# A mixer, cross-attention and expert layer on one core: nine gathered rows in flight where four were, and a pace of 0.7 beside the projections

## The chip, the cores and the metric

The kernel runs on one core of a Trainium2 chip. The metric is the device time of one launch in microseconds (us). Where a text below speaks of "no change", it means a difference of under 0.3%, about 13 us, which is what repeated measurements of this kernel can tell apart.

## The reference

One encoder layer is applied to two groups of tokens, 256 and 1024 of them, with a model width of 1024, all in float32:

```
x = x + W_out [ BiRetention(xn) ; MLA(xn) ]        # xn = RMSNorm(x), one input projection
x = x + MemCrossAttn(RMSNorm(x), RMSNorm(mem))     # 4 heads over 256 memory tokens
x = x + PEER(RMSNorm(x));  y = RMSNorm(x)

def blk(xt):                                        # PEER, for 128 tokens
    q = (xt @ wq).reshape(128, 8, 256)              # 8 heads
    s1, s2 = scores of the two halves of q against 128 sub-keys each
    ...                                             # top 16 of each, top 16 of their sums
    ids, g = the 8 * 16 chosen experts of each token, their softmax
    a = einsum('td,ted->te', xt, U[ids])            # 16384 experts: one row of U, one of V
    return einsum('te,ted->td', g * gelu(a), V[ids])
```

Each token has 128 chosen experts, and each expert is one row of 1024 numbers in U (`peer_u`) and one in V (`peer_v`).

## The kernel before

The 1280 tokens are ten tiles of 128. The stages follow one another: `phase_a` (input projection and retention of all tiles), `phase_b` for the first token block (tiles 0 and 1), with `phase_m` (latent attention) in it, `phase_m` for the second group, `phase_b` for the second and third token block (four tiles each: output projection, cross-attention, expert queries and scores), `gates`, `dense`.

The expert layer is computed in two ways. For six tiles (`DENSE`), `dense` runs over all 16384 experts in 128 blocks of 128 experts. For each block `a_stage` loads the block's rows of U (tiles `ur`, two loads of 256 KB) and V (`vr`, two loads), splits each into a high and a low part (`uh` and `vh` on ScalarE, `ul` and `vl` on GpSimd, four GpSimd instructions a block), multiplies U with the tokens into the PSUM tile `pa` (48 matmuls), applies Gelu (`wr`) and a table of gates (`gt`, 768 KB for two blocks) and splits the result (`wh`, `wl`); every three blocks (`NG`) `v_stage` multiplies it with V into `pv` (36 matmuls a block) and VectorE adds `pv` to `dacc`. The loads `ur` and `vr` share four buffers and are issued by the SP queue.

For the other four tiles (`GATHER`: 0, 1, 8, 9) the generator `gather` fetches just the chosen rows. One step is one indirect DMA issued by GpSimd, which brings one row of U for each of the 128 tokens into a tile `grow` of 128 x 1024 numbers (512 KB), and one VectorE instruction: for U a multiplication with the tokens (`gx`) whose row sum goes to `ga`, for V a multiplication by `ga` and addition to an accumulator. A tile has 128 steps on U and 128 on V, so there are 1024 steps in all. `grow` has four buffers: the fifth row can only be fetched when the first has been used. Once `dense` runs (`self.gps` is set), `banks` copies the tokens and the accumulator to PSUM (tile `gps`); before that they lie in SBUF (`gx`, `gacc`).

What sets the order: `routing` (top 16 lists, VectorE) and `gathering` are queues of generators. `tick(us)` is called behind each group of matmuls with its length and takes steps of them at a share `RHO`: the first number of a pair while there is routing left, the second for gathering. The three pairs belong to the projections (from `phase_m` of the second group on), to `gates` and to `dense`. What is left after `dense` is emitted behind it and depends only on the beginning of `dense`; the scheduler, which runs when the program is built, then sorts instructions of each engine into one fixed order by its own estimate of when each is ready and fits. So the number of buffers of `grow` enters the order of every engine. On the chip each engine follows its order strictly: an instruction that waits holds up all that stand behind it.

The pool `rp` holds the tiles of the routing, the pool `gp` those of the gathering.

Of the kernel before, what the change touches and what calls it, by code (L numbers as in the profile page):

```python
# [10 lines left out]
F32 = mybir.dt.float32  # L11
F32R = mybir.dt.float32r
BF = mybir.dt.bfloat16
# [8 lines left out]
P = 128  # L22
D = 1024
# [23 lines left out]
NG = 3  # L47
O1_BY = "va"

RHO = ((0.75, 0.42), (0.5, 0.0), (0.9, 0.0))  # L50
LATE = 2


SYNC = mybir.DependencyInfo(mybir.DependencyClass.Sync, mybir.DependencyReason.DATA)
# [7 lines left out]
class Lead:  # L62


    def __init__(self, k):
        self.k = k
# [39 lines left out]
class K:  # L106
    def __init__(self, nc, tc, I, O, dbg=None):
        self.nc, self.tc, self.I, self.O = nc, tc, I, O
        self.dbg = dbg or {}
        self.n = 0  # L110
        self.routing, self.gathering = [], []
        self.keeps = []
        self.spare = ()
        self.routed = set()
        self.owed, self.rho = 0.0, (0.0, 0.0)
        self.gps = None
        self.anchor = None
        self.v, self.vf = Lead(self), Fill(self)

    def tick(self, us):  # L120


        rho = self.rho[0 if self.routing else 1]
        if self.rho is RHO[1] and self.routed.issuperset(DENSE):
            rho = 0.0
# [7 lines left out]
    def step(self, q=None):  # L133
        q = q or self.routing or self.gathering
        try:
            return next(q[0])
        except StopIteration:
            q.pop(0)
            return 0.0

    def pace(self, r, ins=None):
# [156 lines left out]
    def phase_a(self, sd):  # L298
# [3 lines left out]
        with ExitStack() as es:  # L302
# [20 lines left out]
            with ExitStack() as e2:  # L323
# [16 lines left out]
                for p in range(RH // 2):  # L340
# [9 lines left out]
                    for t in tiles:  # L350
# [12 lines left out]
                        nc.gpsimd.tensor_tensor(gg[t], gg[t], gw, ALU.mult)  # L363
                        if p and t == LATE:
                            finish()
# [620 lines left out]
    def gather(self, gp, sd, t):  # L986

        nc, I = self.nc, self.I
        v = self.vf

        def row():
            return gp.tile([P, D], F32, tag="grow", name=self.nm("grow"), bufs=4)
        ids = gp.tile([P, P], I32, tag="gids", name=self.nm("gids"), bufs=2)
        nc.sync.dma_start(ids, sd["ids"][t])
        g = gp.tile([P, P], F32, tag="gg", name=self.nm("gg"), bufs=2)
        nc.sync.dma_start(g, sd["g"][t])
        x3 = gp.tile([P, D], F32, tag="gx", name=self.nm("gx"), bufs=1)
        nc.sync.dma_start(x3, sd["x3"][t])
        fw = row()
        nc.sync.dma_start(fw, I["norm_ffn_w"].partition_broadcast(P))  # L1000
        v.tensor_tensor(x3, x3, fw, ALU.mult)
        x3 = self.banks(x3)
        a = gp.tile([P, P], F32, tag="ga", name=self.nm("ga"), bufs=2)

        def rows(src, s):
            u = row()
            nc.gpsimd.indirect_dma_start(out=u, out_offset=None, in_=src,  # L1007
                                         in_offset=bass.IndirectOffsetOnAxis(ap=ids[:, s:s + 1], axis=0))
            return u
        for s in range(P):  # L1010
            u = rows(I["peer_u"], s)
            junk = gp.tile([P, D], BF, tag="gj", name=self.nm("gj"), bufs=1)
            v.scalar_tensor_tensor(junk, u, 1.0, x3, ALU.mult, ALU.mult, accum_out=a[:, s:s + 1])
            yield 1.2
        nc.scalar.activation(a, a, AF.Gelu)
        v.tensor_tensor(a, a, g, ALU.mult)
        acc = gp.tile([P, D], F32, tag="gacc", name=self.nm("gacc"), bufs=1)
        nc.sync.dma_start(acc, sd["x2"][t])
        out, acc = acc, self.banks(acc)
        for s in range(P):  # L1020
            u = rows(I["peer_v"], s)
            v.scalar_tensor_tensor(acc, u, a[:, s:s + 1], acc, ALU.mult, ALU.add)
            yield 1.2
        w = row()
        nc.sync.dma_start(w, I["final_norm_w"].partition_broadcast(P))
        self.finish(gp, t, acc, w, gp.tile([P, D], BF, tag="gj", name=self.nm("gj"), bufs=1), out)

    def banks(self, x):

# [184 lines left out]
    def run(self):  # L1214
        nc, tc, I = self.nc, self.tc, self.I
        with ExitStack() as es:
# [13 lines left out]
            self.setup(cp)  # L1230
            def open_fill():
                self.gp = es.enter_context(tc.tile_pool(name="gp", bufs=1, side="right", reuse_waits="tile"))
                self.rp = es.enter_context(tc.tile_pool(name="rp", bufs=1, side="right", reuse_waits="tile"))
                self.i16 = self.rp.tile([P, 16], BF, name=self.nm("i16"))
                nc.scalar.dma_start(self.i16, I["iota16"])
            self.open_fill = open_fill
            self.phase_a(sd)
            self.phase_b(sd, BLOCKS[:1], lambda: self.phase_m(sd, 0, self.lw))
            self.rho = RHO[0]
            self.phase_m(sd, 1, self.lw)  # L1240
            self.mw.release()
            self.phase_b(sd, BLOCKS[1:])
            self.rho = RHO[1]
            self.dense_inputs(es.enter_context(tc.tile_pool(name="dx", bufs=1, reuse_waits="tile")))
            self.gates(sd)
            self.rho = RHO[2]
            self.gps = es.enter_context(tc.tile_pool(name="gps", bufs=1, reuse_waits="tile", space=PSUM))
            start = self.dense(sd)
            self.anchor = start
            while self.routing or self.gathering:  # L1250
                self.step()

# [73 lines left out]
```

## Time and profile before

| | |
|---|---|
| three runs | 4407.57, 4408.38 (median), 4419.09 us |
| the profiled execution | 4415.91 us, span from first to last instruction 4414.1 us |
| TensorE matmul / weight load busy | 4027.8 us (91%) / 3574.7 us (81%) |
| VectorE, GpSimd, ScalarE busy | 3159.1 us (72%), 2255.5 us (51%), 1643.1 us (37%) |
| moved by DMA | 1030.75 MB, mean 234 GB/s |
| gathers (indirect DMAs) | 512 of U and 512 of V, 545.33 MB |

The shares are means over stages that differ. `dense` with the gathering beside it takes more than half of the span, from about 2075 us to the end. Matmuls are pipelined, so a busy TensorE is not yet one at its best pace: that is read from how many matmuls a stretch holds. The profiled execution's 4415.9 us lie 7.5 us over the median of the three runs.

### The profile page before, as it was taken

How to read it: one execution, taken by the hardware profiler on the slowest of the kernel's cores; microseconds unless marked ns; L12 is line 12 of the kernel's file. 1: busy time of each engine (PE TensorE's matmuls, PEld its weight loads, DVE VectorE, ACT ScalarE, POOL GpSimd, SP SyncE). 2: the span in 40 equal slices, each digit the busy share in tenths (PEclk: the TensorE clock that was granted, in tenths of full speed). 3: DMA queues.
4: the chain of work that ended last, by engine and by line, in shares of the span. 5: the costliest groups of instructions: out<-in, count | busy, mean ns of one | idle time of the engine just before them, and what ended most of it. 6: DMA issues, size and time to landing. Idle time of an engine off the chain costs nothing. (4 is left out here: it accounts for less than half of the span.)

```text
span 4414.1 us, 66568 instructions
## 1 busy us (share of the span) xinstructions
PE 4027.8 (91%) x23202; PEld 3574.7 (81%) x23202; DVE 3159.1 (72%) x7044; ACT 1643.1 (37%) x3570; POOL 2255.5 (51%) x2090
## 2 busy tenths in 40 slices
PE   7999888899898999777999999999999999999998
PEld 7999777667688889666888788888888888888887
DVE  5556422787566696897897777778777777777775
ACT  5333534456343343897322222222222222222223
POOL 2221243012666201676366676777776766677663
PEclk9999999899999999999999999999999999999999
DMA  2112678235778557567488898989998888898884
GB/s 88 36 41 69 210 242 279 69 92 167 249 239 303 181 184 244 169 202 226 157 267 291 279 316 307 315 304 311 317 313 302 307 291 299 303 313 304 298 296 162
DMA packets 489009, 1030.75 MB, mean 234 GB/s; under 512 B 42720, under 2 KB 201952, under 8 KB 488672
## 3 DMA queue, kind: packets, MB, share of 16 engines
q0 software_dynamic: 149536, 545.33, 35.9%
q1 hardware_dynamic: 329200, 470.66, 32.5%
q10 hardware_dynamic: 9936, 10.51, 0.7%
q8 instruction: 182, 2.98, 0.3%
q14 instruction: 155, 1.27, 0.1%
HBM read 901.87 MB, written 124.45 MB: 233 GB/s over the span
## 5 line engine op out<-in xcount | busy, mean ns | idle before, releaser
L1007 POOL DMA_INDIRECT grow<-in_peer_u,gids x512 | 529.3, 1034 | 811.2 <-DVE gj L88 251.2
L88 DVE SCALAR_TENSOR_TENSOR gps<-grow,ga,gps 128x1024 f32<-128x1024 f32 x512 | 658.0, 1285 | 209.0 <-DMA grow<-in_peer_v,gids 203.5
L164 PE MATMUL pa<-dxT,uh 128*128 128x384 f32 x2048 | 692.5, 339 | 37.5 <-ACT wr L1168 32.7
L166 PE MATMUL pa<-dxT,ul 128*128 128x384 f32 x2048 | 684.1, 339 | 7.8 <-POOL ul L1157 7.7
L165 PE MATMUL pa<-dxT,uh 128*128 128x384 f32 x2048 | 690.2, 337 | 0.0
L164 PE MATMUL pv<-vh,wh 128*128 128x512 f32 x1536 | 611.9, 401 | 77.9 <-DVE dacc L72 77.9
L1007 POOL DMA_INDIRECT grow<-in_peer_v,gids x512 | 504.5, 985 | 326.1 <-DVE gps L88 220.4
L165 PE MATMUL pv<-vl,wh 128*128 128x512 f32 x1536 | 616.2, 401 | 17.2 <-POOL vl L1181 16.8
L166 PE MATMUL pv<-vh,wl 128*128 128x512 f32 x1536 | 609.3, 397 | 0.0
L88 DVE SCALAR_TENSOR_TENSOR gj<-grow,gps 128x1024 bf16<-128x1024 f32 x384 | 467.5, 1217 | 194.0 <-DMA grow<-in_peer_u,gids 187.8
L164 PEld LDWEIGHTS pa<-dxT,uh 128*128 128x128 f32 x2048 | 387.9, 189 | 52.7 <-ACT wr L1168 36.7
L164 PEld LDWEIGHTS pv<-vh,wh 128*128 128x128 f32 x1536 | 293.7, 191 | 159.7 <-DVE dacc L72 101.8
L197 POOL TENSOR_TENSOR wl<-wraw,wh 128x512 fp32r<-128x512 f32 x180 | 240.2, 1351 | 345.0 <-ACT wh L193 264.0
L1157 POOL TENSOR_TENSOR ul<-ur,uh 128x512 fp32r<-128x512 f32 x256 | 334.3, 1310 | 155.9 <-ACT uh L1156 150.2
L166 PEld LDWEIGHTS pa<-dxT,ul 128*128 128x128 f32 x2048 | 387.1, 189 | 20.1 <-POOL ul L1157 16.7
L165 PEld LDWEIGHTS pa<-dxT,uh 128*128 128x128 f32 x2048 | 388.0, 189 | 4.3
L165 PEld LDWEIGHTS pv<-vl,wh 128*128 128x128 f32 x1536 | 294.3, 192 | 92.3 <-POOL vl L1181 37.8
L1181 POOL TENSOR_TENSOR vl<-vr,vh 128x512 fp32r<-128x512 f32 x256 | 327.2, 1296 | 67.2 <-ACT vh L1180 64.4
L166 PEld LDWEIGHTS pv<-vh,wl 128*128 128x128 f32 x1536 | 294.5, 192 | 58.0 <-DVE wl L72 0.4
L1156 ACT CAST uh<-ur 128x512 fp32r<-128x512 f32 x256 | 159.0, 621 | 485.9 <-DMA ur<-in_uT 458.4
L164 PE MATMUL pj<-act,wh 128*128 128x256 f32 x1088 | 312.1, 296 | 23.3 <-DVE ld L72 7.2
L72 DVE TENSOR_TENSOR dacc<-pv,dacc 128x1024 f32<-128x1024 f32 x258 | 311.0, 1218 | 25.8 <-PE pv L166 25.5
(282 smaller groups left out, 8969.0 us busy)
## 6 DMA issues: line engine op xcount, KB each, us to landing
ur<-in_uT SPq DMA_DIRECT2D x256, 256.0 KB, 4.0
vr<-in_peer_v SPq DMA_DIRECT2D x256, 256.0 KB, 4.1
G<-st SPq DMA_DIRECT2D x96, 512.0 KB, 6.3
gt<-G SPq DMA_DIRECT2D x64, 768.0 KB, 7.8
wraw<-in_peer_wq SPq DMA_DIRECT2D x96, 256.0 KB, 5.4
wraw<-in_w_out SPq DMA_DIRECT2D x48, 256.0 KB, 4.0
wraw<-in_ca_wq SPq DMA_DIRECT2D x48, 256.0 KB, 3.4
x<-ld SPq DMA_DIRECT2D x24, 512.0 KB, 4.8
```

The costliest lines, as they stand in the source:

```text
L72: r = f(*a, **kw)
L88: r = f(*a, **kw)
L164: mm(ps, a[0], b[0], start=first, stop=False)
L165: mm(ps, a[0], b[1], start=False, stop=False)
L166: mm(ps, a[1], b[0], start=False, stop=last)
L197: (nc.vector if self.spare and k in self.spare else eng).tensor_tensor(wl[:, :n], raw[:, :n], r32(wh[:, :n]), ALU.subtract)
L1007: nc.gpsimd.indirect_dma_start(out=u, out_offset=None, in_=src, in_offset=bass.IndirectOffsetOnAxis(ap=ids[:, s:s + 1], axis=0))
L1156: nc.scalar.copy(uh, ur)
L1157: nc.gpsimd.tensor_tensor(ul, ur, r32(uh), ALU.subtract)
L1181: nc.gpsimd.tensor_tensor(vl, vr, r32(vh), ALU.subtract)
```

## The change

It has three parts. First, once routing is done its pool `rp` is given back and three more rows (`more`) are placed there; and once `dense` has begun (`banked`) the tokens, the accumulator and the finished output have no tiles of their own (`gx`, `gacc`) but use rows like any other, so that the two rooms join the cycle too. Rows are then handed out over nine slots in turn: four `grow`, three `more`, `gx` and `gacc`. Second, the pace of gathering beside the projections goes from 0.42 to 0.7. Third, nothing in the arithmetic changes, but the fixed order of each engine does.

```diff
-RHO = ((0.75, 0.42), (0.5, 0.0), (0.9, 0.0))
+RHO = ((0.75, 0.7), (0.5, 0.0), (0.9, 0.0))
+MORE = 3
...
+        self.slots, self.at = ["grow"] * 4, 0
...
             q.pop(0)
+            if self.gps is not None and not self.routing and self.rp is not None:
+
+                self.rp.release()
+                self.rp = None
+                self.more = self.tc.alloc_tile_pool(name="more", bufs=1, side="right", reuse_waits="tile")
+                self.slots += ["more"] * MORE
             return 0.0
...
+        banked = self.gps is not None
+        if banked and "gx" not in self.slots:
+            self.slots += ["gx", "gacc"]
+
         def row():
-            return gp.tile([P, D], F32, tag="grow", name=self.nm("grow"), bufs=4)
+            self.at += 1
+            tag = self.slots[self.at % len(self.slots)]
+            return (self.more if tag == "more" else gp).tile([P, D], F32, tag=tag, name=self.nm("grow"), bufs=self.slots.count(tag))
+
+        def own(tag):
+            return row() if banked else gp.tile([P, D], F32, tag=tag, name=self.nm(tag), bufs=1)
...
-        x3 = gp.tile([P, D], F32, tag="gx", name=self.nm("gx"), bufs=1)
+        x3 = own("gx")
...
-        acc = gp.tile([P, D], F32, tag="gacc", name=self.nm("gacc"), bufs=1)
+        acc = own("gacc")
...
-        self.finish(gp, t, acc, w, gp.tile([P, D], BF, tag="gj", name=self.nm("gj"), bufs=1), out)
+        self.finish(gp, t, acc, w, gp.tile([P, D], BF, tag="gj", name=self.nm("gj"), bufs=1), row() if banked else out)
```

Counted over the whole order of GpSimd, where two `ul` belong to each of the 128 blocks of `dense`:

| gathers ahead of | before | changed |
|---|---|---|
| the 1st `ul` (block 0) | 131 | 212 |
| the 33rd `ul` (block 16) | 189 | 264 |
| the 197th `ul` (block 98) | 807 | 1014 |
| the last gather stands behind | `ul` 252 | `ul` 199 |

On VectorE, 115 gathered rows are used ahead of the third token block's first `wl` before, 178 in the changed kernel; 127 and 208 ahead of the first instruction of `gates`. The first tile's 128 rows of V are all added up in SBUF (`gacc`) in the changed kernel, in PSUM (`gps`) before.

The next two pieces show GpSimd's order late in `dense`; the number behind a name tells tiles apart, `ul` and `vl` are the low parts of U and V, `grow` is a gathered row. Before, in the expert blocks 102 and 103:

```order
L1157 TENSOR_TENSOR ul_37598<-ur_37595,uh_37597 128x512
L1007 DMA grow_43695<-in_peer_u,gids_43370 128x1024
L1157 TENSOR_TENSOR ul_37604<-ur_37601,uh_37603 128x512
L1007 DMA grow_43699<-in_peer_u,gids_43370 128x1024
L1181 TENSOR_TENSOR vl_37674<-vr_37671,vh_37673 128x512
L1007 DMA grow_43703<-in_peer_u,gids_43370 128x1024
L1157 TENSOR_TENSOR ul_37686<-ur_37683,uh_37685 128x512
L1007 DMA grow_43707<-in_peer_u,gids_43370 128x1024
L1157 TENSOR_TENSOR ul_37692<-ur_37689,uh_37691 128x512
```

And in the changed kernel, in blocks 99 to 102, from the last two gathers of all on:

```order
L1025 DMA grow_44283<-in_peer_v,gids_43373 128x1024
L1025 DMA grow_44286<-in_peer_v,gids_43373 128x1024
L1175 TENSOR_TENSOR ul_37467<-ur_37464,uh_37466 128x512
L1199 TENSOR_TENSOR vl_37537<-vr_37534,vh_37536 128x512
L1175 TENSOR_TENSOR ul_37551<-ur_37548,uh_37550 128x512
L1175 TENSOR_TENSOR ul_37557<-ur_37554,uh_37556 128x512
L1175 TENSOR_TENSOR ul_37639<-ur_37636,uh_37638 128x512
L1175 TENSOR_TENSOR ul_37645<-ur_37642,uh_37644 128x512
L1199 TENSOR_TENSOR vl_37543<-vr_37540,vh_37542 128x512
```

The gathers that stood between the splits have moved ahead, and the last 28 blocks hold none.

The second place is VectorE's order in the third token block of the projections, where it computes the weights' low parts `wl`; `ld` and `act` are the tokens on their way to the matmuls, `tv`, `ti`, `rs`, `oh` belong to the routing. Before:

```order
L72 TENSOR_TENSOR ld_16356<-pj_16708,ld_16356 128x512
L88 MAX_INDEX ti_16685<-tv_16684,rs_16686 128x8 x2
L88 TENSOR_TENSOR ii_16401<-oh_16647 128x64
L88 MAX_INDEX ti_16685<-tv_16684,rs_16686 128x8
L197 TENSOR_TENSOR wl_16833<-wraw_16830,wh_16832 128x512
L88 MATCH_REPLACE rs_16686<-tv_16684,rs_16686 128x128 x3
L88 MAX tv_16684<-rs_16686 128x8
L197 TENSOR_TENSOR wl_16839<-wraw_16836,wh_16838 128x512
```

In the changed kernel:

```order
L74 TENSOR_SCALAR ld_16594<-ld_16594,rs_17039 128x1024
L74 RECIPROCAL rs_17045<-rs_17045 128x1
L206 TENSOR_TENSOR wl_17097<-wraw_17094,wh_17096 128x512
L90 SCALAR_TENSOR_TENSOR gacc_14688<-grow_16329,ga_11155,gacc_14688 128x1024
L90 MAX_INDEX ti_16952<-tv_16951,rs_16953 128x8 x4
L74 SCALAR_TENSOR_TENSOR act_17052<-tr_17106,c_normw,act_17051 128x256
L90 TENSOR_TENSOR oh_16799<-oh_16799 128x64x4
L206 TENSOR_TENSOR wl_17103<-wraw_17100,wh_17102 128x512
```

A gathered row's addition to `gacc` now stands among the weights and the routing, where there was none.

## Rows read from the trace of the kernel before

**Rows 1.** Windows: stretch, length, PE, PEld, DVE, ACT, POOL busy, clock, DMA share, GB/s

```profile
945.00:1450.00 505.00, 456.90 (x2932) 383.48 (x2929) 334.52 (x651) 227.78 (x485) 257.33 (x206) 0.96 0.70 232
1500.00:1700.00 200.00, 178.29 (x1191) 164.36 (x1190) 186.40 (x891) 93.09 (x223) 6.77 (x7) 0.94 0.60 205
2350.00:3825.00 1475.00, 1395.07 (x6828) 1239.90 (x6827) 1131.74 (x1410) 375.32 (x678) 1021.80 (x943) 0.98 0.88 305
4350.00:4400.00 50.00, 50.00 (x245) 44.19 (x244) 19.04 (x23) 16.09 (x28) 12.35 (x10) 1.00 0.18 61
```

**Rows 2.** Timeline of PE: start, us, instruction; first and last of two unbroken runs

```profile
4351.71 0.39 PE L166 MATMUL pv<-vh,wl 128*128 128x512 f32 x1
...
4355.11 0.39 PE L166 MATMUL pv<-vh,wl 128*128 128x512 f32 x1
...
4361.19 0.33 PE L164 MATMUL pa<-dxT,uh 128*128 128x384 f32 x1
...
4363.97 0.34 PE L165 MATMUL pa<-dxT,uh 128*128 128x384 f32 x1
```

**Rows 3.** Windows of the matmuls into `pa` alone, then of those into `pv`

```profile
2350.00:3825.00 1475.00, 714.36 (x3903) 0.98 0.88 305
...
2350.00:3825.00 1475.00, 725.23 (x2925) 0.98 0.88 305
```

**Rows 4.** Groups of VectorE, 2350 to 3825: busy, mean ns, idle before and releasers

```profile
L88 DVE SCALAR_TENSOR_TENSOR gps<-grow,ga,gps 128x1024 f32<-128x1024 f32 x325 | 417.8, 1285 | 143.1 <-DMA grow<-in_peer_v,gids 139.4
L88 DVE SCALAR_TENSOR_TENSOR gj<-grow,gps 128x1024 bf16<-128x1024 f32 x292 | 355.4, 1217 | 145.3 <-DMA grow<-in_peer_u,gids 140.0 <-ACT gps L1034 2.6 <-DVE gj L88 0.4
...
L88 DVE DVE_READ_ACCUMULATOR gj<-grow,gps 128x1 f32 x292 | 23.9, 82 | 0.0
```

**Rows 5.** Waits, 2350 to 3825: who for whom, us in total, times, longest

```profile
POOL grow L1007 <- DVE gps L88: 160.6, 146, 7.3
...
POOL grow L1007 <- DVE gj L88: 126.4, 135, 5.0
...
PE pv L164 <- DVE dacc L72: 47.3, 35, 3.4
...
PE pv L165 <- POOL vl L1181: 11.2, 24, 1.4
```

**Rows 6.** Groups of GpSimd, 2350 to 3825; then one row of its timeline

```profile
L1007 POOL DMA_INDIRECT grow<-in_peer_v,gids x322 | 313.9, 975 | 191.6 <-DVE gps L88 142.0 <-issue 24.3 <-DMA grow<-in_peer_v,gids 12.2
...
L1157 POOL TENSOR_TENSOR ul<-ur,uh 128x512 fp32r<-128x512 f32 x164 | 213.4, 1305 | 67.1 <-ACT uh L1156 65.1
...
2617.48 0.94 POOL L1007 DMA_INDIRECT grow<-in_peer_u,gids  x1 [0.30 <-issue]
```

**Rows 7.** DMA, 2350 to 3825: gathers' queue, then issues with us to landing

```profile
q0 software_dynamic: 88832, 323.48, 63.1%
...
ur<-in_uT SPq DMA_DIRECT2D x163, 256.0 KB, 4.0
...
grow<-in_peer_u,gids POOLq DMA_INDIRECT x295, 5.6
```

**Rows 8.** Windows of 10 to 15 us with full DMA; last two columns share, GB/s

```profile
1380.00:1395.00 15.00, 12.75 (x92) 12.35 (x91) 12.60 (x39) 3.17 (x8) 7.96 (x6) 0.89 1.04 401
...
3650.00:3660.00 10.00, 10.00 (x55) 9.54 (x55) 5.70 (x8) 1.03 (x3) 5.16 (x6) 1.00 0.99 362
3870.00:3880.00 10.00, 10.00 (x54) 9.24 (x53) 7.22 (x15) 3.17 (x6) 8.09 (x8) 1.00 0.98 331
```

**Rows 9.** Windows of cross-attention to scores, second and third block; then gather issues

```profile
1203.00:1465.00 262.00, 239.90 (x1705) 225.36 (x1703) 155.27 (x328) 103.74 (x249) 161.47 (x127) 0.96 0.79 264
1528.00:1773.00 245.00, 230.10 (x1667) 217.99 (x1666) 195.15 (x945) 98.61 (x237) 13.03 (x12) 0.97 0.59 200
...
1203.00:1465.00 262.00, 73.41 (x60) 0.96 0.79 264
```

**Rows 10.** Groups of VectorE, 945 to 1450: a gathered row used out of SBUF

```profile
L88 DVE SCALAR_TENSOR_TENSOR gj<-grow,gx 128x1024 bf16<-128x1024 f32 x115 | 177.2, 1540 | 17.3 <-DMA grow<-in_peer_u,gids 16.4
```

More of the change, by code (lines that the diff above doesn't have):

```diff
@@ L115, in __init__ @@
         self.owed, self.rho = 0.0, (0.0, 0.0)
-        self.gps = None
+        self.gps = self.rp = None
+        self.slots, self.at = ["grow"] * 4, 0
         self.anchor = None
@@ L1232, in open_fill @@
                 self.gp = es.enter_context(tc.tile_pool(name="gp", bufs=1, side="right", reuse_waits="tile"))
-                self.rp = es.enter_context(tc.tile_pool(name="rp", bufs=1, side="right", reuse_waits="tile"))
+                self.rp = tc.alloc_tile_pool(name="rp", bufs=1, side="right", reuse_waits="tile")
                 self.i16 = self.rp.tile([P, 16], BF, name=self.nm("i16"))
@@ L1251, in run @@
                 self.step()
+            self.more.release()
 def layout(inp):
```

## The prediction, made before the changed kernel ran

> **What bounds the kernel now.** I read the windows by stage first. With gathers beside the experts, from 2350 to 3825 us, TensorE is busy for 1395 of 1475 us; from 4350 us on, with none, for 50 of 50 [rows 1]. Busy is not pace, so the next view is the timeline where nothing interrupts: 15 steps into `pv` take 3.40 us, 16 into `pa` 2.78 us, so one costs 0.2267 and 0.1738 us [rows 2]. A block of 128 experts has 48 and 36 of them: 8.34 + 8.16 = 16.50 us, TensorE's floor. The stretch held 3903 and 2925 [rows 3], which is 81.3 blocks and 1341 us of floor: 134 us, 9%, are lost, at 18.1 us a block.
>
> The groups of VectorE say why. It used 617 gathered rows there, one in 2.39 us, and stood idle for 143.1 + 145.3 us, nearly all until a row had landed [rows 4]. In the waits GpSimd holds the next gather for 160.6 + 126.4 us until VectorE has used a row [rows 5]: the two wait for each other, since only four rows go round. Four times 2.39 is 9.6 us a turn, of which 5.6 us is the landing [rows 7], 1.0 the issue [rows 6] and 1.3 the use [rows 4]. TensorE gets the bill late: 47.3 us until VectorE had added up `pv`, 11.2 us until GpSimd had split V [rows 5]. So latency bounds the gathers, their rate sets the order, and TensorE loses a little everywhere.
>
> **The change, part by part.** The fixed order puts 75 more gathers ahead of block 16, 207 more ahead of block 98, and none behind block 99. So there are three terms.
>
> *Blocks 98 to the end, without gathers.* This began at about 3825 us and took 589 us to 4414. What remains there is 30 blocks of `pa` and, since `pv` trails by three, 33 of `pv`: 30 x 8.34 + 33 x 8.16 = 520 us, and about 8 us to finish. Alone, TensorE runs at its floor [rows 1]; at 98% of it this is 538 us, **-51 us**. Bounds: -61 at the floor, -34 at 95%.
>
> *Blocks 16 to 98, with 750 gathers, not 618.* Nine rows for one gather in 1.9 us leave 17 us a turn, so latency is no longer the limit. Each resource is, nearly. TensorE's floor: 82 x 16.5 = 1353 us. VectorE: a row costs 1.285 (V) or 1.217 + 0.082 us (U), 1.29 on average; its other work is 1131.7 - 797 = 335 us in 81.3 blocks, 4.12 a block [rows 1, 4]; 750 x 1.29 + 82 x 4.12 = 1306 us. GpSimd: 0.98 us a gather and 0.30 between two, 1.30 for each of four splits [rows 6]: 750 x 1.28 + 82 x 5.2 = 1386 us. DMA: 305 GB/s x 1475 us = 450 MB moved, of which 323.5 by gathers [rows 1, 7]; 132 gathers more of 0.524 MB make 519 MB. Where the DMA engines were full for 10 to 15 us they moved 331, 362 and 401 GB/s [rows 8], so 1568, 1434 or 1294 us. I take the middle, at which DMA is the last of four close limits, and 6 us for their getting in each other's way: 1440 us for 1475, **-35 us**. Bounds: 1390 us, just over GpSimd's sum (-85), and 1568 us (+93).
>
> The Trainium skill ("DMA: Bandwidth & Descriptors", Specifications) gives about 358 GB/s as the limit of HBM for a core. Fifteen microseconds at 401 GB/s in this trace [rows 8] are over it; by that figure the stretch would take an estimated 1450 us, and the large gain below would be out.
>
> *The projections, 81 gathers more.* Of these, 63 go where 115 were, ahead of the third token block, 18 into that block, which had 12. The nearest price: from cross-attention to scores the second block took 262 us with 60 gathers, the third 245 us with 12 [rows 9], the same matmuls; all 17 us put down to 60 gathers makes 0.28 us each. The other bound is VectorE's full time, 1.54 us out of SBUF [rows 10] and 0.08 for the row sum: 1.62 us. From 1500 to 1700 us VectorE is busy for 186 of 200 [rows 1], so nothing covers it there; from 945 to 1450 it is busy for 335 of 505, which does. I take 63 x 0.28 + 18 x 1.62 = **+47 us**, bounds +23 and +131. The landings there get longer too, at a DMA share of 0.70 [rows 1], which is within the upper bound.
>
> In that stretch the same multiplication costs 1540 ns with the tokens in SBUF, for 1217 ns with them in PSUM in `dense` [rows 4, 10]. The Trainium skill ("GPSIMD Engine Reference", Key points) says that GpSimd shares its SBUF interfaces with VectorE and that VectorE's instructions with two SBUF inputs contend with it, which agrees. It speaks against the change: the first tile's 128 rows of V are now added up in SBUF, not in PSUM, most of them beside the projections. That extra 0.3 us a row is in the 1.62 us.
>
> *What costs nothing.* Up to block 16 there are 52 gathers for 58, still over four rows in the main: no change. The three rows in the routing's room wait until routing has ended; in the fixed order GpSimd's `ul` and `vl` stand behind such a gather, and TensorE for those. The cover is the splits made ahead, one block and a half of `uh` and `ul`, 25 us; without it, once, about a turn of a row, 9.6 us. The tokens and sums of the last three tiles are now loaded into rows, by SP, in whose queue `ur` and `vr` stand behind; four such buffers hold one block, 16.5 us, and `ur` lands in 4.0 us [rows 7], so a few us of waiting, a dozen times, are hidden.
>
> The sum: -51 - 35 + 47 = -39 us on the profiled execution's 4415.9 us, 4377 us. That execution lies 7.5 us above the median, so in its terms **4370 us**, 0.9% faster.
>
> **The rivals**, all in terms of the median, 4408 us.
>
> *All limits give way* (16%). Deep queues let DMA run at 401 GB/s, and gathers beside the projections cost 0.28 us each: -85 - 61 + 23 = -123, 4285 us. For: the 401 GB/s were reached with two full queues. Against: GpSimd would need every gap.
>
> *DMA is the wall already* (17%). Its share is 0.88 at 305 GB/s [rows 1]; if that is proportional, 347 GB/s is all there is, the stretch takes 519 / 347 = 1496 us (+21), and waiting for a free row becomes waiting for bytes. With -51 and +23 to +47: -7 to +17, so 4401 to 4425, about 4412 us: no change, or just slower.
>
> *The projections pay in full* (15%). VectorE has no room and weights come late behind gathers: +131 - 35 - 51 = +45, 4453 us. It decides from 86 / 81 = 1.06 us for a gather on; the traces' 0.28 speaks against, the crowded third block for it.
>
> *Dense in lockstep falls behind* (10%). Runs of gathers on VectorE and GpSimd, at a DMA rate of 331 GB/s, hold back `dacc` and `vl`, and TensorE waits more than the 47 us: +93 - 51 + 47 = +89, 4497 us.
>
> **How the numbers follow.** My case has 42%, with its own range 4340 to 4400. Faster by over 0.3% (13 us): 40 of these, the 16 of the large gain and 1 of the wall, 57%. Within 0.3%: 2 and 12 of the wall, 14%. Slower: 4 of the wall, 15 and 10, 29%. The range has to reach from most of the way to the large gain to just beyond the projections' price: 4295 to 4460 us leaves out about 10 in a hundred at either end.
>
> **What would show it.** Right: the stretch from the last gather on at 16.5 us a block with DMA nearly idle; VectorE's wait for landing rows well under 288 us in the gathered stretch, at 340 GB/s or more; GpSimd's waits for VectorE nearly gone; the projections up to the gates some 50 us longer. Wrong: a DMA share near 1 at under 350 GB/s with landing times of 15 us; waits of `pv` for `dacc` above 50 us in the stretch; the third token block longer by 40 us or more; or TensorE at less than 95% of its pace behind the last gather, so that something other than gathers took the 9%.

## The result, and the profile after

The changed kernel took 4464.65 us (median of four runs, 4460.79 to 4466.65), the kernel before, run beside it, 4409.6 us: a ratio of 1.0123 (95% interval 1.0106 to 1.014). It is 1.2% slower, where 0.9% faster was predicted. Its profiled span is 4462.0 us, for 4414.1.

To see where the 48 us between the two spans arose (the medians lie 55 us apart), equal work has to be compared, not equal times. The matmuls into `pa` and `pv`, counted from 2040 us on and weighted with 0.1738 and 0.2267 us [rows 2], say how far the expert blocks have come. These windows count them in the changed kernel, first into `pa`, then into `pv` (stretch, length, TensorE busy and matmuls, clock, DMA share, GB/s):

```profile
2040.00:2415.00 375.00, 151.57 (x797) 0.95 0.67 215
2040.00:3925.00 1885.00, 890.41 (x4680) 0.97 0.88 313
...
2040.00:2415.00 375.00, 126.19 (x494) 0.95 0.67 215
2040.00:3925.00 1885.00, 853.30 (x3424) 0.97 0.88 313
```

And in the kernel before:

```profile
2040.00:2359.00 319.00, 148.93 (x810) 0.97 0.69 223
2040.00:3833.00 1793.00, 863.87 (x4716) 0.98 0.85 290
...
2040.00:2359.00 319.00, 121.73 (x482) 0.97 0.69 223
2040.00:3833.00 1793.00, 845.05 (x3399) 0.98 0.85 290
```

797 x 0.1738 + 494 x 0.2267 = 250 us of TensorE's floor are done at 2415 us after and, by 810 and 482, at 2359 before: about block 16, 56 us late. At 1590 us of floor, about block 98, it is 3925 against 3833. In the same way 20 us of floor, some 110 matmuls into block 0, are reached at 2148 and 2102. So the parts are:

| part | before | after | difference | predicted |
|---|---|---|---|---|
| to the beginning of block 0 | 2102 | 2148 | +46 | +47 |
| blocks 0 to 16 | 257 | 267 | +10 | 0 |
| blocks 16 to 98, "the stretch" below (1340 us of floor) | 1474 | 1510 | **+36** | **-35** |
| from there to the end | 581 | 537 | -44 | -51 |

Windows of all engines in the changed kernel (columns as in [rows 1]): cross-attention to scores of the second token block, the passage to the third, the third; then the stretch, and what follows the last gathers:

```profile
943.00:1489.00 546.00, 481.79 (x3040) 403.14 (x3036) 402.88 (x717) 234.12 (x498) 325.14 (x261) 0.93 0.80 266
1489.00:1570.00 81.00, 58.53 (x266) 47.37 (x265) 76.42 (x218) 24.18 (x47) 37.18 (x33) 0.87 0.84 295
1570.00:1826.00 256.00, 235.86 (x1669) 220.32 (x1666) 213.77 (x985) 98.80 (x236) 19.97 (x20) 0.96 0.62 211
...
2415.00:3925.00 1510.00, 1407.66 (x6815) 1248.60 (x6814) 1335.05 (x1607) 353.76 (x669) 1137.70 (x1060) 0.97 0.94 338
...
3946.00:4411.00 465.00, 463.29 (x2349) 422.71 (x2348) 154.91 (x187) 129.47 (x234) 154.09 (x122) 1.00 0.32 101
```

The same matmuls before, which correspond to the first four of these:

```profile
945.00:1465.00 520.00, 471.90 (x3041) 397.69 (x3038) 334.52 (x651) 233.93 (x497) 266.16 (x213) 0.96 0.69 229
1465.00:1528.00 63.00, 53.70 (x267) 45.28 (x266) 58.34 (x243) 23.63 (x45) 8.87 (x7) 0.92 0.56 188
1528.00:1773.00 245.00, 230.10 (x1667) 217.99 (x1666) 195.15 (x945) 98.61 (x237) 13.03 (x12) 0.97 0.59 200
...
2359.00:3833.00 1474.00, 1394.07 (x6825) 1239.23 (x6824) 1132.49 (x1412) 376.35 (x680) 1022.18 (x942) 0.98 0.88 305
```

The matmul counts agree to three in the projections and to ten in the stretch; the lengths are 26, 18 and 11 us more in the projections. In the stretch the DMA share rose from 0.88 to 0.94 and the rate from 305 to 338 GB/s, and it still took longer: 338 x 1510 = 510 MB for 450. Of the 36 us more, TensorE stood idle for 22; for the other 14 it was busy longer with the same matmuls, at a mean granted clock of 0.97 for 0.98.

What VectorE did there (answering to [rows 4], columns as there):

```profile
L90 DVE SCALAR_TENSOR_TENSOR gps<-grow,ga,gps 128x1024 f32<-128x1024 f32 x359 | 461.3, 1285 | 8.0 <-ACT gps L1052 0.8
L90 DVE SCALAR_TENSOR_TENSOR gj<-grow,gps 128x1024 bf16<-128x1024 f32 x376 | 457.2, 1216 | 8.4 <-ACT gps L1052 1.3
```

And the waits in the stretch (answering to [rows 5]):

```profile
ACT wr L1186 <- PE pa L175: 703.5, 117, 15.5
POOL grow L1025 <- DVE gps L90: 135.2, 188, 4.1
...
POOL grow L1025 <- DVE gj L90: 103.0, 144, 4.4
DVE wr L74 <- ACT wr L1186: 101.8, 70, 5.5
...
PE pa L175 <- POOL ul L1175: 52.8, 23, 5.4
...
PE pv L173 <- DVE dacc L74: 20.0, 23, 2.5
```

Two of these, from the same work in the kernel before (2359 to 3833 us):

```profile
ACT wr L1168 <- PE pa L166: 184.1, 98, 6.6
...
PE pa L166 <- POOL ul L1157: 4.0, 10, 0.6
```

VectorE's idle time ahead of a row fell from 288 to 16 us: the wait that nine rows were to remove is gone. But TensorE now waits 52.8 us for `ul`, where it waited 4.0 before, GpSimd still waits 238 us for VectorE to free a row, and ScalarE waits 703.5 us for TensorE ahead of `wr`, for 184.1. Loads take longer to land (answering to [rows 7]; the queue's packets, MB and share, then issues with us to landing):

```profile
q0 software_dynamic: 106033, 386.12, 70.1%
...
ur<-in_uT SPq DMA_DIRECT2D x161, 256.0 KB, 5.0
grow<-in_peer_u,gids POOLq DMA_INDIRECT x369, 6.4
```

`ur` needs 5.0 us, not 4.0, a gather of U 6.4, not 5.6. Whether it is these landings that TensorE waits for can be read from one of its longest stops. GpSimd's timeline (start, us, instruction, idle before):

```profile
3104.14 1.32 POOL L1175 TENSOR_TENSOR ul<-ur,uh 128x512 fp32r<-128x512 f32 x1
3105.61 0.95 POOL L1025 DMA_INDIRECT grow<-in_peer_u,gids  x1 [0.16 <-issue]
...
3113.09 0.94 POOL L1025 DMA_INDIRECT grow<-in_peer_u,gids  x1 [0.30 <-DVE gj L90]
3114.05 1.27 POOL L1175 TENSOR_TENSOR ul<-ur,uh 128x512 fp32r<-128x512 f32 x1
```

ScalarE's, where it makes the `uh` that the second of these `ul` needs:

```profile
3103.07 0.62 ACT L1174 CAST uh<-ur 128x512 fp32r<-128x512 f32 x1 [4.73 <-POOL vl L1199]
```

And TensorE's there:

```profile
3109.61 0.34 PE L174 MATMUL pa<-dxT,uh 128*128 128x384 f32 x1
3115.38 0.69 PE L175 MATMUL pa<-dxT,ul 128*128 128x384 f32 x1 [5.43 <-POOL ul L1175]
```

Seven gathers stand in GpSimd's fixed order between two `ul`, at 1.25 us each; TensorE has run through what had been split and stops for 5.43 us. The landing is not what it waits for here: `uh` was ready at 3103.69, TensorE had already multiplied with it by 3109.61, and the `ul` came 10.4 us after `uh` because GpSimd was at other work. The stretch has 23 such waits for `ul`; in each of the twelve that last over 2 us, the `uh` had been ready for 6.3 us or more.

A stop costs more than it lasts. Behind this one the granted clock of TensorE is at its lower level, 1.2 GHz, and 5 us hold 18 matmuls in place of 29 (columns as in [rows 1]):

```profile
3116.00:3121.00 5.00, 5.00 (x18) 5.00 (x17) 1.50 (x1) 0.49 (x1) 4.65 (x5) 0.50 1.00 381
3122.00:3127.00 5.00, 5.00 (x29) 4.83 (x28) 4.97 (x10) 2.93 (x6) 2.75 (x4) 1.00 0.97 310
```

### The profile page after: what moved, and what is told of

The parts are those of the page before. It is cut to its first block, busy times and chain, and to the rows that moved or that the text cites. A ratio compares the mean times of both kernels' runs of the same rounds, so it can differ in the third digit from the quotient of the medians.

```text
span 4462.0 us, 66577 instructions
## 1 busy us (share of the span) xinstructions
PE 4051.5 (91%) x23202; PEld 3597.7 (81%) x23202; DVE 3248.6 (73%) x7044; ACT 1627.3 (36%) x3569; POOL 2292.1 (51%) x2090
## 4 chain that ended last, share of the span: by engine, by line
PE 27%; POOL 9%; issue 8%; DVE 6%; DMA 2%; ACT 1%; SPq 0%; POOLq 0%; DVEq 0%; ACTq 0%
POOL grow L1025 6%; PE pa L175 5%; PE pa L173 4%; PE pa L174 4%; PE pv L173 4%; PE pv L174 4%; PE pv L175 4%; DVE gps L90 2%; POOL ul L1175 2%; POOL vl L1199 1%; DVE gj L90 1%; DVE dacc L74 1%; DVE wr L74 1%; DVE oh L90 1%; DMA ur<-in_uT 1%
## 5 line engine op out<-in xcount | busy, mean ns | idle before, releaser
L1025 POOL DMA_INDIRECT grow<-in_peer_v,gids x512 | 517.2, 1010 | 478.1 <-DVE tv L90 153.1
L173 PE MATMUL pa<-dxT,uh 128*128 128x384 f32 x2048 | 699.2, 341 | 15.2 <-ACT wr L1186 10.8
L174 PE MATMUL pa<-dxT,uh 128*128 128x384 f32 x2048 | 698.8, 341 | 0.0
L90 DVE SCALAR_TENSOR_TENSOR gps<-grow,ga,gps 128x1024 f32<-128x1024 f32 x384 | 493.4, 1285 | 8.5 <-ACT gps L1052 0.8
L1199 POOL TENSOR_TENSOR vl<-vr,vh 128x512 fp32r<-128x512 f32 x256 | 337.1, 1334 | 273.1 <-ACT vh L1198 271.2
L1186 ACT ACTIVATE wr<-pa 128x384 f32<-128x384 f32 x256 | 125.4, 491 | 902.0 <-PE pa L175 895.5
L173 PEld LDWEIGHTS pa<-dxT,uh 128*128 128x128 f32 x2048 | 394.5, 193 | 28.1 <-ACT wr L1186 11.6
L174 PEld LDWEIGHTS pa<-dxT,uh 128*128 128x128 f32 x2048 | 394.0, 192 | 6.1
L74 DVE TENSOR_TENSOR wr<-wr,gt 128x384 f32<-128x384 f32 x256 | 180.4, 705 | 277.1 <-ACT wr L1186 255.5
```

Of the source, the lines that this page charges most:

```text
L74: r = f(*a, **kw)
L90: r = f(*a, **kw)
L173: mm(ps, a[0], b[0], start=first, stop=False)
L174: mm(ps, a[0], b[1], start=False, stop=False)
L1186: nc.scalar.activation(wr, ps[:, :H], AF.Gelu)
L1199: nc.gpsimd.tensor_tensor(vl, vr, r32(vh), ALU.subtract)
```

## The experiments

Two theories were set against each other. **A:** at nine gathers a block DMA has too many bytes to bring, and everything is late behind it. **B:** the engines in their fixed orders hold one another up (GpSimd's time and its runs of gathers ahead of `ul`, or VectorE's time), whatever DMA does. Of every run the stretch is taken as above, between 250 and 1590 us of floor. The last column tells of ScalarE's fixed order in the stretch, counted in the trace: the share of the `uh` that stand ahead of both `wr` of the block before, so that U is split a whole block ahead. Most of the others stand behind both, and a `wr` waits for TensorE.

| kernel | median us, ratio to before (interval) | stretch us | gathers a block there | GB/s, share | `uh` a block ahead |
|---|---|---|---|---|---|
| before | | 1474 | 7.6 | 305, 0.88 | 0.50 |
| changed | 4464.65, 1.0123 (1.0106 to 1.014) | 1510 | 9.1 | 338, 0.94 | 0.16 |
| e1: nine rows, pace 0.42 | 4419.76, 1.001 (0.9993 to 1.0026) | 1514 | 8.7 | 329, 0.92 | 0.18 |
| e2: four rows, pace 0.7 | 4467.66, 1.0109 (1.0088 to 1.0131) | 1476 | 7.6 | 303, 0.88 | 0.49 |
| e3: nine, 0.42, 0.6 beside `dense` | 4318.37, 0.978 (0.9764 to 0.9796) | 1424 | 7.7 | 318, 0.89 | 0.36 |
| e4: changed, no `ul` | 4415.3 (one run) | 1466 | 9.0 | 346, 0.94 | 0.20 |
| e5: nine, 0.7, 0.55 beside `dense` | 4378.05, 0.9914 (0.9889 to 0.9939) | 1412 | 7.2 | 304, 0.86 | 0.45 |
| e6: nine, 0.25, 0.65 beside `dense` | 4353.44, 0.9879 (0.9856 to 0.9903) | 1447 | 8.4 | 333, 0.92 | 0.25 |
| e7: changed, half rows by DMA | 4340.12 (one run) | 1407 | 9.1 | 227, 0.73 | 0.49 |
| e8: changed, half rows by VectorE | 4462.57 (one run) | 1541 | 9.2 | 336, 0.93 | 0.07 |
| e9: four, 0.42, 0.6 beside `dense` | 4410.24, 0.9995 (0.9985 to 1.0005) | 1468 | 7.6 | 306, 0.88 | 0.50 |
| e10: seven, 0.42, 0.6 beside `dense` | 4330.16, 0.9823 (0.9789 to 0.9856) | 1436 | 7.8 | 319, 0.89 | 0.35 |
| e11: nine, 0.42, 0.55 beside `dense` | 4395.88, 0.9965 (0.9952 to 0.9979) | 1429 | 7.1 | 298, 0.84 | 0.46 |
| e12: changed, four `uh`, `ul` buffers | 4467.94, 1.0142 (1.0118 to 1.0166) | 1513 | 9.1 | 339, 0.94 | 0.21 |

**The two parts of the change, each alone.** e1 has the nine rows and the old pace, e2 the four rows and the new one:

```diff
 e1, against the changed kernel
-RHO = ((0.75, 0.7), (0.5, 0.0), (0.9, 0.0))
+RHO = ((0.75, 0.42), (0.5, 0.0), (0.9, 0.0))
 e2, against the kernel before
-RHO = ((0.75, 0.42), (0.5, 0.0), (0.9, 0.0))
+RHO = ((0.75, 0.7), (0.5, 0.0), (0.9, 0.0))
```

> The changed kernel with the pace beside the projections put back to 0.42; nine rows stay. The order then has 131 gathers ahead of the experts' pass, as before, nearly nine a block in it, and none behind block 110 of 128. If the dense gathering itself is what failed (lockstep of GpSimd and VectorE, or full DMA), the projections give back their 46 us, the gathered stretch still runs at about 2.0 us a gather and 18.5 us a block, and some 18 blocks at the end run at TensorE's floor: about 4395 us against 4410 of before. If the whole loss came from the pace, and nine rows are neither good nor bad: 4410 to 4420 us. If nine rows are good by themselves: 4340 to 4370 us.

> The kernel before with the pace beside the projections raised to 0.7; four rows stay. 212 gathers ahead of the experts' pass, none behind block 116. If the pace alone costs the projections what the changed kernel showed there, the experts' pass begins 46 us later than before, and 12 blocks at TensorE's floor at the end give back about 20 us: 4435 us. If the projections were slow for the rows out of SBUF or for the other part of the change, it begins within 20 us of before: about 4400 us.

e1 came out like the kernel before, e2 like the changed one, not at the 4435 us expected. The pace alone costs the whole loss: in e2 block 0 begins 55 us later than before (81 gathers at 0.7 us), and the blocks behind the stretch give back 15, not 20. The nine rows alone give nothing. Windows of the stretch of e1 and then of e2:

```profile
2351.00:3865.00 1514.00, 1402.62 (x6819) 1245.36 (x6819) 1318.33 (x1594) 358.87 (x679) 1110.75 (x1034) 0.98 0.92 329
```

```profile
2427.00:3903.00 1476.00, 1396.21 (x6825) 1237.10 (x6824) 1128.72 (x1481) 369.82 (x671) 1022.03 (x945) 0.98 0.88 303
```

With nine rows the stretch is 40 us longer than with four at the old pace, 34 us at the new one; the blocks behind it, soon without gathers, give back 22 and 29 of these.

**The same nine rows, spread.** In e3 the third pair's second number, which is 0 in both kernels, is 0.6, so that gathers beside `dense` are taken at a share of TensorE's time instead of as early as the scheduler can place them. e9 is the same with four rows.

```diff
 e3, against the changed kernel
-RHO = ((0.75, 0.7), (0.5, 0.0), (0.9, 0.0))
+RHO = ((0.75, 0.42), (0.5, 0.0), (0.9, 0.6))
 e9, against the kernel before
-RHO = ((0.75, 0.42), (0.5, 0.0), (0.9, 0.0))
+RHO = ((0.75, 0.42), (0.5, 0.0), (0.9, 0.6))
```

> Nine rows, pace 0.42 beside the projections and 0.6 in the experts' pass, so that the gathers are spread over all blocks, 7.7 a block and not 9.1. If the loss in the changed kernel comes from too many gathers a block for engines that each follow a fixed order (or for the DMA engines, at 337 GB/s), TensorE's loss in the pass falls to half of the 9% of before and VectorE hardly waits for rows to land: 4330 to 4360 us. If four rows and their latency were never what cost TensorE its 9%, the time stays at 4400 to 4415 us.

> Four rows as before, pace 0.42 beside the projections as before, but a share of 0.6 instead of 0 beside dense. Theory (four rows are held to their rate by the wait for a free row, so a share beside dense has nothing to spread): 131 gathers ahead of the first block and the last behind the 252nd ul, as before; 4395 to 4420 us, no difference from before. Rival (the gain of 90 us in the kernel with nine rows and a share of 0.6 came from the share and the other order of the engines, not from the rows): 4320 to 4350 us.

e3 is 2.2% faster than the kernel before, e9 no different from it. The two have nearly the same gathers a block, the same bytes and the same order of stages, and the stretch takes 1424 us with nine rows, 1468 with four. The groups of VectorE say what is saved, in e3 (2346 to 3770 us):

```profile
L90 DVE SCALAR_TENSOR_TENSOR gps<-grow,ga,gps 128x1024 f32<-128x1024 f32 x321 | 412.2, 1284 | 5.5
L90 DVE SCALAR_TENSOR_TENSOR gj<-grow,gps 128x1024 bf16<-128x1024 f32 x302 | 367.0, 1215 | 9.5 <-ACT gps L1052 2.5 <-DMA grow<-in_peer_u,gids 2.2
```

and in e9 (2357 to 3825 us):

```profile
L88 DVE SCALAR_TENSOR_TENSOR gps<-grow,ga,gps 128x1024 f32<-128x1024 f32 x321 | 412.5, 1285 | 144.9 <-DMA grow<-in_peer_v,gids 142.2
L88 DVE SCALAR_TENSOR_TENSOR gj<-grow,gps 128x1024 bf16<-128x1024 f32 x296 | 360.2, 1217 | 151.1 <-DMA grow<-in_peer_u,gids 146.1 <-ACT gps L1034 2.6
```

296 us of waiting for rows became 15, and TensorE's wait for `dacc` fell with it, from 46.7 to 8.0 us. So the wait of [rows 4] was a real cost, and removing it is worth about 45 us in the stretch, as long as the gathers are not also moved closer together. That is half of the 88 us between the two spans: another 33 us arise behind the stretch (550 us for 583), where e9 has gathers nearly to the end.

**What stops nine gathers a block.** e4, e7 and e8 keep the changed kernel's pace and rows and relieve one resource each: GpSimd of one split in two, DMA of half of each gathered row, VectorE of half of its work on a row. e12 gives TensorE more cover against a late `ul`.

```diff
 e4
...
-                        nc.gpsimd.tensor_tensor(ul, ur, r32(uh), ALU.subtract)
-                        U.append((uh, ul))
+                        U.append((uh, uh))
 e7
-            nc.gpsimd.indirect_dma_start(out=u, out_offset=None, in_=src,
+            nc.gpsimd.indirect_dma_start(out=u[:, 0:512], out_offset=None, in_=src.rearrange("e (h d) -> (e h) d", h=2),
...
-            return u
+            return u[:, 0:512].unsqueeze(1).broadcast_to([P, 2, 512])
...
 e8
-            v.scalar_tensor_tensor(junk, u, 1.0, x3, ALU.mult, ALU.mult, accum_out=a[:, s:s + 1])
+            v.scalar_tensor_tensor(junk[:, 0:512], u[:, 0:512], 1.0, x3[:, 0:512], ALU.mult, ALU.mult, accum_out=a[:, s:s + 1])
...
-            v.scalar_tensor_tensor(acc, u, a[:, s:s + 1], acc, ALU.mult, ALU.add)
+            v.scalar_tensor_tensor(acc[:, 0:512], u[:, 0:512], a[:, s:s + 1], acc[:, 0:512], ALU.mult, ALU.add)
 e12
-                        uh = dx.tile([P, 4, P], F32R, tag="uh", name=self.nm("uh"), bufs=3)
-                        ul = dx.tile([P, 4, P], F32R, tag="ul", name=self.nm("ul"), bufs=3)
+                        uh = dx.tile([P, 4, P], F32R, tag="uh", name=self.nm("uh"), bufs=4)
+                        ul = dx.tile([P, 4, P], F32R, tag="ul", name=self.nm("ul"), bufs=4)
...
-                        wh = ap.tile([P, H], F32R, tag="wh", name=self.nm("wh"), bufs=2 * NG + 3)
+                        wh = ap.tile([P, H], F32R, tag="wh", name=self.nm("wh"), bufs=2 * NG + 2)
-                        wl = ap.tile([P, H], F32R, tag="wl", name=self.nm("wl"), bufs=2 * NG + 3)
+                        wl = ap.tile([P, H], F32R, tag="wl", name=self.nm("wl"), bufs=2 * NG + 2)
```

> The changed kernel without the 256 GpSimd instructions that make the low part of U; the matmuls that read it read the high part in its place, so the result differs. Gathers, VectorE's work and DMA are as in the changed kernel. Lockstep through GpSimd's queue (splits stand behind gathers that wait for VectorE to free a row): TensorE's waits for GpSimd, 65 us in the gathered stretch, mostly go, and the stretch, 1515 us, falls below 1460 us. Full DMA or a full VectorE: the stretch stays within 20 us of 1515.

> The changed kernel, but each gather fetches 512 of a row's 1024 numbers and VectorE reads these twice, so that its work is the same; the result differs. Full DMA as the limit: the stretch from block 16 to 98, 1500 us in the changed kernel by TensorE's finished work, falls below 1440 us. Lockstep of GpSimd and VectorE, or a full VectorE: it stays between 1470 and 1530 us, with DMA at about 200 GB/s.

> The changed kernel, but VectorE uses 512 of a gathered row's 1024 numbers, so that its time for a row is about halved; the DMA fetches whole rows and the result differs. VectorE as the pacing engine of the lockstep: the stretch from block 16 to 98 falls from 1500 to 1400 to 1430 us and DMA goes above 350 GB/s. Full DMA at 340 GB/s: it stays at 1500 us, and VectorE waits for rows to land again.

> The changed kernel (nine rows, 0.7) with four uh and four ul buffers where there are three, so that two blocks of split U can be made ahead, not one and a half; wh and wl give up one buffer each of nine for the room. Gathers per block as in the changed kernel (212 ahead of block 0, 1024 by block 99). Theory A (the bytes of nine gathers a block beside the block's own loads are what DMA cannot bring any faster): the gathered stretch stays at 1490 to 1510 us, DMA at about 337 GB/s, total 4455 to 4475 us. Theory B (runs of gathers ahead of ul in GpSimd's queue stop TensorE, and cover would help): the stretch falls by 30 us or more, total under 4435 us, TensorE's wait for ul gone.

Windows of the stretch in e7, columns as before:

```profile
2399.00:3806.00 1407.00, 1371.06 (x6821) 1221.13 (x6820) 1338.97 (x1613) 369.08 (x672) 1162.56 (x1067) 1.00 0.73 227
```

and its landings:

```profile
ur<-in_uT SPq DMA_DIRECT2D x163, 256.0 KB, 3.0
grow<-in_peer_v,gids POOLq DMA_INDIRECT x376, 3.8
```

In e7 VectorE is busier than in any other run (0.95 of the time), GpSimd issues as many gathers, and TensorE gets through the stretch 103 us sooner, at 1407 us, the shortest of all and below the 1440 that A had set. It stands idle for 66 us less, and is busy for 37 us less with the same matmuls, at a granted clock of 1.00 for 0.97. In e7 the engines do keep up with nine gathers a block. In e8,

```profile
2388.00:3929.00 1541.00, 1415.49 (x6823) 1259.96 (x6822) 926.15 (x1619) 360.10 (x681) 1136.22 (x1072) 0.96 0.93 336
```

VectorE is busy for 0.60 of the time and the stretch is 31 us longer, at nearly the same rate of DMA. That is neither of the two outcomes expected: it did not get shorter, and VectorE hardly waits for rows to land. In e12 the total is as A had it, and TensorE waits for `ul` as in the changed kernel,

```profile
PE pa L175 <- POOL ul L1175: 53.6, 21, 4.7
```

for the changed kernel's 52.8, while in e7 it fell to 9.3 us. In e4 that wait is gone, since there is no `ul`; TensorE waits 49.0 us for `dacc` instead of 20.0, and the stretch is 44 us shorter, at 346 GB/s:

```profile
2405.00:3871.00 1466.00, 1386.85 (x6811) 1239.66 (x6810) 1290.99 (x1607) 353.37 (x666) 924.41 (x893) 0.98 0.94 346
```

This too lies between what the two theories gave, below 1460 and 1495 to 1535 us.

For A speaks that the four kernels with nine gathers a block and full rows stay at 336 to 346 GB/s and a share of 0.93 or 0.94, whichever engine is relieved, and that only fewer bytes bring the stretch near its floor. For B speaks that 213 us less of GpSimd's work gave 44 us, and that TensorE's waits for `ul` arise in GpSimd's order, behind `uh` that lie ready.

Neither is proved, because each of the four edits also gave the engines another fixed order, and with seven or nine rows the last column of the table follows the stretch more closely than the share of DMA does. In e7, the only fast kernel with nine gathers a block, `uh` is back a block ahead (0.49), and ScalarE's wait for TensorE ahead of `wr` is back too,

```profile
ACT wr L1187 <- PE pa L175: 192.1, 88, 5.8
```

for 703.5 us. In e12 the buffers for more cover were there, but the order hardly used them (0.21), so it does not test the cover. In e8 there was less cover still (0.07), and between blocks 16 and 98 GpSimd's order has 72 runs of six or more gathers, for the changed kernel's 35 and e7's 41, so it does not test VectorE's time alone. In the changed kernel 21 of the 23 waits for `ul` fell on a block whose `uh` stands behind both `wr`. Whether e7 is fast for its bytes, for the shorter landings that come with them, or for its order, no run tells; it would take nine gathers a block with whole rows in the order of e7.

**How close the gathers may stand.** e5, e6 and e11 vary the two paces, e10 the rows (`MORE = 1`, otherwise as e3).

```diff
 e5, e6, e11, against the changed kernel
-RHO = ((0.75, 0.7), (0.5, 0.0), (0.9, 0.0))
+RHO = ((0.75, 0.7), (0.5, 0.0), (0.9, 0.55))
+RHO = ((0.75, 0.25), (0.5, 0.0), (0.9, 0.65))
+RHO = ((0.75, 0.42), (0.5, 0.0), (0.9, 0.55))
```

> The changed kernel with one difference: a pace of 0.55 for the gathers in the experts' pass, so that they are spread over blocks 8 to 123 at 7 a block and not 9.1 up to block 99. The pace beside the projections stays at 0.7. If crowding is what failed in the pass and the pace costs the projections about 50 us whatever follows: the pass begins 46 to 56 us later than in the kernel before, but loses no more than 5% to TensorE's floor: 4360 us. If spreading helped only because the pace was lower too: 4440 us or more.

> Nine rows, a pace of 0.25 beside the projections and 0.65 in the experts' pass: 81 gathers ahead of the pass and 8.4 a block in it. At 0.69 us a gather (56 us for 81 in the four-row kernel) the projections give back 35 us against pace 0.42; 50 gathers more go into the pass. If a block takes 8.4 as well as 7.7: 4290 us. If crowding sets in there: 4320 to 4350 us.

> The spread kernel (0.42 beside the projections, 0.6 beside dense) with one row in the room of routing, not three: seven in turn. Theory (at one gather in some 2.15 us and 8 us from a gather's issue to its row's use four rows are just too few, and anything from five on is enough): 4315 to 4330 us, as with nine. Rival (deep queues as such make the gain, each row adds to it): halfway between four and nine or worse, 4345 to 4380 us.

> Nine rows, 0.42 beside the projections, 0.55 instead of 0.6 beside dense: 190 gathers ahead of block 16, 757 ahead of block 96, the last behind the 256th ul, so some 7.1 a block instead of 7.7 and a remainder behind the last block. Theory (below some 320 GB/s the gathers cost TensorE little per block, so the stretch gets nearer to its floor, and the gathers left over at the end are the price): delay in the stretch 10 to 20 us less than at 0.6, total 4310 to 4350 us with a remainder of 10 to 40 us in which TensorE idles. Rival (the fewer a block the better, the remainder is hidden): under 4305 us.

With nine rows the stretch takes 1429, 1412, 1424, 1447, 1514 and 1510 us at 7.1, 7.2, 7.7, 8.4, 8.7 and 9.1 gathers a block: flat up to 7.7, and steep from 8.4 on. The last two points are also the two kernels with a share of 0 beside `dense`, and with the density the share of `uh` that stand a block ahead falls from 0.46 to 0.16, so these runs don't separate the density from the order that comes with it. e5 has the changed kernel's start (81 gathers early, 54 us late at block 0) and is still faster than the kernel before, because its stretch is 62 us shorter than there, 98 us shorter than in the changed kernel; its 4378 us are above the 4360 expected. e6 went the other way, 50 gathers fewer beside the projections than e3: that gave back 21 us there (block 0 began 33 us earlier than in the kernel before, in e3 12 us), and cost more in `dense`. Seven rows (e10) are nearly as good as nine; 4330 us is at the edge of what was expected, and the two intervals overlap. In e11 the gathers ran out too late: 51 were left behind the last `ul`, and TensorE stood still beside them,

```profile
4350.00:4375.00 25.00, 0.00 (x0) 0.00 (x0) 24.34 (x20) 0.00 (x0) 17.63 (x20) 0.50 1.02 408
```

so that the stretch was as good as in e3 and what followed it 63 us longer (613 us to the end, 550 in e3); 10 to 40 us had been expected for that, and a stretch 10 to 20 us shorter. e3 remains the fastest kernel.

## Why the prediction was wrong

**The step that failed is the term "Blocks 16 to 98, with 750 gathers, not 618": predicted -35 us, measured +36.** Its first half was right: with nine rows latency is no longer the limit (VectorE's 288 us of waiting for rows are 16). Its second half chose 362 GB/s, "the middle, at which DMA is the last of four close limits", and 6 us for their getting in each other's way. In the run DMA moved 510 MB, close to the 519 of the sum, at 338 GB/s. At a share of 0.94 this is 338 / 0.94 = 360 GB/s of a full DMA, so the rate of a full DMA was well taken. What was wrong is that it would be full, with 6 us for four close limits: at 360 GB/s the 510 MB would have taken 1417 us, and the stretch took 93 us more. In none of the fourteen kernels did the share over the stretch exceed 0.94. A second wrong step stands under "What costs nothing": the cover of one block and a half of `uh` and `ul` was there in buffers, but the changed order put only 0.16 of the `uh` a block ahead, for 0.50 before, and TensorE's wait for `ul` grew from 4.0 to 52.8 us. How far the bytes and how far the orders cause this stays open, as said above.

The wall that the second rival named, 347 GB/s and 1496 us, was nearest to the measured 1510; it had 17%. The total, 4464.65 us, lies just above the range of 4295 to 4460 and nearest to the rival of 4453, but not in the way of that rival: its projections were to cost 131 us, and cost 46.

The sum also counted 132 gathers that move out of the last blocks as a gain there, without a price where they go, other than through the bytes. By the runs with nine rows the price is steep, if all of the difference is put down to the number: 1510 - 1424 us for 736 - 624 gathers (e3), 0.77 us each, while the last blocks gained 44 us by 207 gathers fewer, 0.21 us each.

**Blocks 98 to the end: right.** -44 us for -51; between 3946 and 4411 us TensorE is busy for 463 of 465 us at a DMA share of 0.32. The 537 us to the end are within a microsecond of the predicted 538.

**The projections: the sum right, its parts not.** +46 us for +47, so that the sum came out by luck. The 0.28 us a gather had divided the 17 us by the second block's 60 gathers; the third has 12, so 48 is the difference, and 0.35 the price by these windows, which with 1705 and 1667 matmuls [rows 9] do not hold quite the same work. The gathers cost 0.5 to 0.8 us in the second block and the passage to the third alike (26 us for 51 of them, 18 us for 22), not 0.28, and the third block 11 us for 8; `gates` gave 7 us back (266 us for 273). VectorE's sums in SBUF took 1539 ns on average between 943 and 1826 us, where those in PSUM take 1285 in the stretch. But this mean, like the 1540 of [rows 10], is not what one of them takes (ns, shortest, median and longest: sums in SBUF and in PSUM in the changed kernel, then products in SBUF before, from 945 to 1450):

```profile
L90 DVE SCALAR_TENSOR_TENSOR gacc<-grow,ga,gacc x80: 1258/1279/4561, 1340.8 to 1778.7; 128x1024 f32<-128x1024 f32 x80
...
L90 DVE SCALAR_TENSOR_TENSOR gps<-grow,ga,gps x359: 1271/1290/1291, 2646.3 to 3922.6; 128x1024 f32<-128x1024 f32 x180
...
L88 DVE SCALAR_TENSOR_TENSOR gj<-grow,gx x115: 1204/1220/6155, 946.0 to 1429.7; 128x1024 bf16<-128x1024 f32 x115
```

Of the 80 sums in SBUF, the 54 that run while GpSimd splits nothing take 1276 ns on average, none over 1347; the 26 that overlap a split take 2085. In PSUM no such difference is seen. So the prediction's 0.3 us a row are the price of a split beside it, not of SBUF.

**Blocks 0 to 16: wrong by 10 us.** e2 has +13 there with four rows, e1 -4 with nine, so it belongs to the pace and not to the rows; why was not followed up.

**The other signs.** "GpSimd's waits for VectorE nearly gone" was wrong: 238 us remain of 287. GpSimd then waits for rows that VectorE has not yet used. As far as the waits tell, this is because `wr` comes late from TensorE (101.8 us) and stands ahead of rows in VectorE's order. "340 GB/s or more" was missed by two. Of the signs of error, a DMA share near 1 below 350 GB/s came true, with landings of 6 us, not 15; `pv`'s wait for `dacc` fell, to 20 us. The rival of the lockstep, with 4497 us, took `dacc` and `vl` for what TensorE would wait for; it was `ul`. The Trainium skill ("DMA: Bandwidth & Descriptors", Specifications) gives about 358 GB/s as the limit of HBM for a core, and says further down, under its measured bandwidths, that each core gets about this much when both cores of a domain stream. This launch uses one core. Over the stretch no run here was above 346; over 25 us with nothing but gathers, e11 moved 408 GB/s, so 358 is not a limit here.

What stays open: how the 170 us between the changed kernel's stretch and its floor divide between bytes, landing times, GpSimd's time and the fixed orders, beyond the 103 us that went with halving the rows and the 44 that leaving out `ul` did, which need not add up; and why the stretch gets so much longer between 8.4 and 8.7 gathers a block, where the DMA share is 0.92 in both and the `uh` a block ahead are 0.25 and 0.18.

## What to carry to other kernels

Deeper buffering removes a wait, but it also lets a scheduler that places work "as early as it fits" pack that work closer, and the denser stretch can lose what the wait had cost: here the same nine rows gave nothing or 2.2%, depending on one share that spread them. Where the program is put in order by a scheduler, an edit that halves an instruction moves others too: count the new order before putting the time down to the resource that was relieved. When several resources of a stretch are each computed to be 90 to 97% full, don't take the fullest at its full rate: count its measured share (0.93 to 0.94 was the most here) and compare with the rate that a control at lower density shows. And a change made of two parts is worth costing apart: its slower half here was the pace, 0.6 to 0.7 us per gather brought forward, which the other half did not touch.

## What the runs showed of the hardware

DMA's rate at full share depends on what is in it: 408 GB/s at a share of 1.02 with gathers alone (e11), and 338 / 0.94 = 360 GB/s where gathers of 4 KB rows run beside the blocks' loads. Landing times lengthen long before that: `ur` 3.0, 4.0 and 5.0 us, gathers 3.8 (of half rows), 5.6 and 6.4 us at 227, 305 and 338 GB/s.

A VectorE instruction that reads a row and its second operand from SBUF takes 1276 ns here while GpSimd splits nothing and 2085 on average beside a split (up to 4561); with the second operand in PSUM it takes 1271 to 1291 ns either way.

After TensorE had stood still for 5.43 us, its granted clock was 0.50, and one matmul followed another after 0.32 us, not 0.17. Over the stretch the mean granted clock runs from 0.96 in e8, the longest, to 1.00 in e7, the shortest.
